# The low part of w_up: a ScalarE negation and an accumulating transfer in place of a VectorE subtraction

## The chip, the cores and the metric

The kernel runs on one core of one Trainium2 chip. The metric is the device time of one launch in microseconds (us), lower is better. Before the change it is 2234.87 us, the median of 3 runs (2234.61 to 2236.42).

## What is computed

One layer of a hybrid decoder on 512 tokens of width 2048, all in float32. Cut to what matters here:

```python
h = rmsnorm(x, norm1_w)
proj = h @ w_in                      # split among three groups of mixers
y = concat(stick_breaking(6 heads), short_conv(4 groups), gated_delta(6 heads))
x = x + y @ w_out
h2 = rmsnorm(x, norm2_w)
x = x + square(relu(h2 @ w_up)) @ w_down     # w_up: 2048 x 8192, w_down: 8192 x 2048
return rmsnorm(x, final_norm_w)
```

## The kernel before, in words

**Products of split numbers.** Every float32 operand of a large product is split into a high part (rounded to float32r by a ScalarE copy) and a low part (the rest: VectorE subtracts the high part from the operand). A product is then three matmuls into one PSUM bank, in `mm3` (L106): high times high (L108), high weight times low activation (L109), low weight times high activation (L110).

**Loading weights.** `wload` (L96 to L104) does this for w_in, w_out and w_up, in pieces of 128 x 512, 256 KB each, 2 KB in each partition: a transfer on SP's queue into `raw` (L99), the copy on ScalarE that writes `whi` (L102), the subtraction on VectorE that writes `wlo` (L103). Each of the three tiles has four buffers. So the high part for a piece can be written when the piece four before it has been through L109, and `raw` is free again when L103 has read it. The whole of `wload` is put 400 places forward in the planner's priority.

**Stages.** From 0 to about 545 us of the span: the first projections and the gated delta heads. To about 760 us: attention. To about 911 us: x + y @ w_out (L734 to L754), 16 columns of 4 pieces each; per column one GpSimd addition of squares (L750) is made towards the norm. Then w_up: a row tile f of 128 features needs four pieces (`up_chunk`, L760), each 12 matmuls; after the fourth, VectorE (L775) and ScalarE (L776) take the squared ReLU. The first 16 pieces (L782 to L789) come one right after the other, but for the transposes of `turn` (L729) and the sum over partitions of the squares (L785), which needs the last L750. Then, until about 2180 us, each block of 16 pieces is interleaved with 14 units of the w_down product (L913 to L919): a piece, a unit, a piece, a unit, and two pieces without a unit at the end of a block. A unit is a Strassen-like product of 12 matmuls as well; its weights `q` come on SP's queue (L839, 512 KB each), are combined on VectorE (L848) and split on ScalarE (L806) and VectorE (L807); its results are added on VectorE (L876). The last 53 us are the last block of w_down, the final norm and the output.

**Order.** Each engine runs its instructions in an order fixed when the program is built. The planner orders them by a simulated timeline and by the priorities. SP's queue carries the loads of `raw` and of `q`. GpSimd (POOL) carries the additions of L750 in the w_out stage, the last multiplications (L952), and nothing between 955 and 2180 us.

Of the kernel before, what the change touches and what calls it, by code (L numbers as in the profile page):

```python
# [11 lines left out]
F32 = mybir.dt.float32  # L12
F32R = mybir.dt.float32r
AF = mybir.ActivationFunctionType
ALU = mybir.AluOpType

P = 128
# [10 lines left out]
CHUNK_KT = 4  # L28
# [25 lines left out]
def trunk(ctx, tc, xT, wv1, wv2, wa, wo, wu, wd, vec, wf, out, dbg=None):  # L54
    nc = tc.nc
    V, S, G, PE = nc.vector, nc.scalar, nc.gpsimd, nc.tensor
# [15 lines left out]
    def mmps():  # L72
        pool, bufs = pool_of_mm
        return pool.tile([P, 512], F32, name="mm", tag="mm", bufs=bufs)

    def xps(tag):
        pool, bufs = pool_of[tag]
        return pool.tile([P, 512], F32, name=tag, tag=tag, bufs=bufs)
# [8 lines left out]
    def tmp(n=512):  # L87
        return per.tile([P, n], F32, name="tmp", tag="tmp", bufs=4)
# [4 lines left out]
    def f32t(shape, name):  # L93
        return per.tile(shape, F32, name=name)

    def wload(src, n, prio=None):  # L96
        with tc.high_priority(WPRIO if prio is None else prio):
            raw = per.tile([P, 512], F32, name="raw", tag="raw", bufs=4)
            nc.sync.dma_start(out=raw[:, :n], in_=src)  # L99
            hi = per.tile([P, 512], F32R, name="whi", tag="whi", bufs=4, align_bytes=256)  # L100
            lo = per.tile([P, 512], F32R, name="wlo", tag="wlo", bufs=4, align_bytes=256)
            S.copy(out=hi[:, :n], in_=raw[:, :n])  # L102
            V.tensor_tensor(out=lo[:, :n], in0=raw[:, :n], in1=hi[:, :n].bitcast(F32), op=ALU.subtract)  # L103
        return hi, lo  # L104

    def mm3(p, lh, ll, rh, rl, first, last, more=False):  # L106

        PE.matmul(p, lhsT=lh, rhs=rh, start=first, stop=False, skip_group_check=more)  # L108
        PE.matmul(p, lhsT=lh, rhs=rl, start=False, stop=False, skip_group_check=more)  # L109
        PE.matmul(p, lhsT=ll, rhs=rh, start=False, stop=last, skip_group_check=more)  # L110

    def gemm(src, acts, ts=slice(0, T)):

        p = mmps()[:, :ts.stop - ts.start]
        nk = len(acts)
        for c in range(0, nk, CHUNK_KT):
            hi, lo = wload(src[:, c:c + CHUNK_KT, :].rearrange("p k f -> p (k f)"), CHUNK_KT * P)
            for k in range(CHUNK_KT):
                s = slice(k * P, (k + 1) * P)
                a = acts[c + k]  # L120
                mm3(p, hi[:, s], lo[:, s], a[:, 0, ts], a[:, 1, ts], c + k == 0, c + k == nk - 1)
        return p
# [59 lines left out]
    for k in range(KT):  # L182
        hi, lo = wload(wv1[:, k, :], 268, 0)
        xr = big_pool.tile([P, 512], F32, name="xr", tag="xr", bufs=3)
        nc.sync.dma_start(out=xr, in_=xT[:, k, :])
        a = big()
        w = col(C_N1 + k)
        S.activation(out=a[:, 0], in_=xr, func=AF.Copy, scale=w)
        V.scalar_tensor_tensor(out=a[:, 1], in0=xr, scalar=w, in1=a[:, 0].bitcast(F32),
                               op0=ALU.mult, op1=ALU.subtract)  # L190
        for b in range(NB):
            s = slice(b * P, (b + 1) * P)
            mm3x = v1p[b][:, :268]
            PE.matmul(mm3x, lhsT=a[:, 0, s], rhs=hi[:, :268], start=k == 0, stop=False)
            PE.matmul(mm3x, lhsT=a[:, 0, s], rhs=lo[:, :268], start=False, stop=False)
            PE.matmul(mm3x, lhsT=a[:, 1, s], rhs=hi[:, :268], start=False, stop=k == KT - 1)
        if k == 0:
            S.activation(out=acc, in_=xr, func=AF.Square)
        else:
            sq = tmp()  # L200
            if k % 2:
                V.tensor_tensor(out=sq, in0=xr, in1=xr, op=ALU.mult)
            else:
                S.activation(out=sq, in_=xr, func=AF.Square)
            G.tensor_tensor(out=acc, in0=acc, in1=sq, op=ALU.add)
        xw.append(a)
    R = pt([P, 512], "R")
    p = xps("r")
# [3 lines left out]
    p = xps("r")  # L212
# [44 lines left out]
    def v_stage(i):  # L257
        pp = [mmps(), mmps()]
        for c in range(0, KT, 2):
            hi, lo = wload(wv2[i - 1][:, c:c + 2, :].rearrange("p k f -> p (k f)"), 512)  # L260
            for kk in range(2):
                k = c + kk
                ws = slice(kk * 256, kk * 256 + 256)
                for b in range(NB):
                    s = slice(b * P, (b + 1) * P)
                    o = pp[b // 2][:, (b % 2) * 256:(b % 2) * 256 + 256]
                    PE.matmul(o, lhsT=xw[k][:, 0, s], rhs=hi[:, ws], start=k == 0 and b % 2 == 0, stop=False)  # L267
                    PE.matmul(o, lhsT=xw[k][:, 0, s], rhs=lo[:, ws], start=False, stop=False)  # L268
                    PE.matmul(o, lhsT=xw[k][:, 1, s], rhs=hi[:, ws], start=False, stop=k == KT - 1 and b % 2 == 1)  # L269
        vt[i] = v_evac(lambda b: pp[b // 2][:, (b % 2) * 256:(b % 2) * 256 + 256], sp_pool)  # L270
# [32 lines left out]
    p = xps("r")  # L303
# [430 lines left out]
    for m in range(KT):  # L734
        xr = big_pool.tile([P, 512], F32, name="xr", tag="xr", bufs=3)
        nc.sync.dma_start(out=xr, in_=xT[:, m, :])
        p = gemm(wo[m], yh)
# [22 lines left out]
    def up_chunk(f, c, st):  # L760

        if c == 0:
            st["p"] = mmps()
        p = st["p"]
        hi, lo = wload(wu[f][:, c * CHUNK_KT:(c + 1) * CHUNK_KT, :].rearrange("p k f -> p (k f)"), CHUNK_KT * P)
        for k in range(CHUNK_KT):
            s = slice(k * P, (k + 1) * P)
            a = xw2[c * CHUNK_KT + k]
            mm3(p, hi[:, s], lo[:, s], a[:, 0], a[:, 1], c + k == 0, c == KT // CHUNK_KT - 1 and k == CHUNK_KT - 1)
        if c == KT // CHUNK_KT - 1:  # L770
            g = f // HK
            if f % HK == 0:
                hp[g] = late.tile([P, HK, 512], F32, name="hp", tag="hp", bufs=3)
            t = tmp()
            V.scalar_tensor_tensor(out=t, in0=p, scalar=0.0, in1=Rb, op0=ALU.max, op1=ALU.mult)  # L775
            S.activation(out=hp[g][:, f % HK], in_=t, func=AF.Square)  # L776
# [5 lines left out]
    for n in range(FBLK * NCH):  # L782
        if n == 1:
            p = xps("r")
            PE.matmul(p, lhsT=ones, rhs=acc2, start=True, stop=True)  # L785
            rsqrt_exp(Rb, p, 1.0 / D, None)
        if n == 2:
            turn(KT - 2)
        up_chunk(n // NCH, n % NCH, ust)  # L789
# [123 lines left out]
    for b in range(nblk - 1):  # L913
        for n in range(FBLK * NCH):
            up_chunk((b + 1) * FBLK + n // NCH, n % NCH, ust)
            if n < 14:
                if n % 7 == 0:
                    dst = {}
                unit(b, n // 7, PROD[n % 7], dst)  # L919
# [110 lines left out]
```

## Time and profile before

| | |
|---|---|
| median of 3 runs | 2234.87 us (2234.61 to 2236.42) |
| the profiled execution: own time | 2235.26 us |
| its span, first to last instruction | 2233.3 us |
| TensorE (PE) busy | 2206.4 us, 99% |
| VectorE (DVE) busy | 1618.9 us, 72% |
| ScalarE (ACT) busy | 943.9 us, 42% |
| GpSimd (POOL) busy | 90.8 us, 4% |
| mean granted clock of TensorE | 0.997 |

Busy times are sums over the span. PE is matmuls, PEld the loading of their weights, which runs beside them. In a row of a group of instructions, the number after x counts them, the two after the first bar are their busy time in us and the mean of one in ns, and after the second bar stands the idle time of the engine just before them and what ended most of it. A releaser written `<-PE mm L109` means that the engine waited for that.

### The profile page before, as it was taken

How to read it: one execution, taken by the hardware profiler on the slowest of the kernel's cores; microseconds unless marked ns; L12 is line 12 of the kernel's file. 1: busy time of each engine (PE TensorE's matmuls, PEld its weight loads, DVE VectorE, ACT ScalarE, POOL GpSimd, SP SyncE). 2: the span in 40 equal slices, each digit the busy share in tenths (PEclk: the TensorE clock that was granted, in tenths of full speed). 3: DMA queues.
4: the chain of work that ended last, by engine and by line, in shares of the span. 5: the costliest groups of instructions: out<-in, count | busy, mean ns of one | idle time of the engine just before them, and what ended most of it. 6: DMA issues, size and time to landing. Idle time of an engine off the chain costs nothing.

```text
span 2233.3 us, 28056 instructions
## 1 busy us (share of the span) xinstructions
PE 2206.4 (99%) x10394; PEld 1831.8 (82%) x10394; DVE 1618.9 (72%) x2262; ACT 943.9 (42%) x1563; POOL 90.8 (4%) x126
## 2 busy tenths in 40 slices
PE   7999999999999999999999999999999999999998
PEld 6887888878988888888888888888888888888886
DVE  7787999754657633477787777778878878778774
ACT  5645655433435433433343333333333433333334
POOL 4000000000000111000000000000000000000003
PEclk9999999999999999999999999999999999999999
DMA  6332323322222333433333333343333332333432
GB/s 185 98 94 83 87 80 91 86 79 85 81 85 81 108 114 113 141 98 117 97 101 115 92 109 109 90 118 99 90 123 94 99 113 90 113 104 93 118 111 79
DMA packets 112505, 227.06 MB, mean 102 GB/s; under 512 B 18448, under 2 KB 20624, under 8 KB 112368
## 3 DMA queue, kind: packets, MB, share of 16 engines
q1 hardware_dynamic: 112368, 225.26, 34.2%
q8 instruction: 82, 1.34, 0.3%
q14 instruction: 55, 0.45, 0.1%
HBM read 218.53 MB, written 6.68 MB: 101 GB/s over the span
## 4 chain that ended last, share of the span: by engine, by line
PE 93%; DVE 4%; DMA 1%; issue 1%; ACT 1%; SPq 0%; ACTq 0%; DVEq 0%
PE mm L108 20%; PE mm L109 20%; PE mm L110 20%; PE pp L108 9%; PE pp L110 9%; PE pp L109 9%; DVE wlo L103 1%; PE mm L269 1%; PE mm L268 1%; PE mm L267 1%; DVE Yq L432 1%; DVE tq L430 1%; DVE cv L337 0%; DMA xr<-in_xT_dram 0%; PE i L391 0%
## 5 line engine op out<-in xcount | busy, mean ns | idle before, releaser
L102 ACT CAST whi<-raw 128x512 fp32r<-128x512 f32 (+1 forms) x544 | 333.1, 613 | 622.6 <-PE mm L109 579.3
L103 DVE TENSOR_TENSOR wlo<-raw,whi 128x512 fp32r<-128x512 f32 (+1 forms) x544 | 374.1, 688 | 246.3 <-ACT whi L102 234.0
L876 DVE TENSOR_TENSOR xq<-pp,xq 128x1024 f32<-128x1024 f32 x240 | 290.8, 1222 | 203.0 <-PE pp L110 200.5
L108 PE MATMUL mm<-big,whi 128*128 128x512 f32 x1024 | 404.7, 396 | 0.0
L110 PE MATMUL mm<-big,wlo 128*128 128x512 f32 x1024 | 403.5, 394 | 0.0
L109 PE MATMUL mm<-big,whi 128*128 128x512 f32 x1024 | 403.3, 394 | 0.0
L108 PE MATMUL mm<-xw,whi 128*128 128x512 f32 x1024 | 398.8, 389 | 0.0
L110 PE MATMUL mm<-xw,wlo 128*128 128x512 f32 x1024 | 398.4, 389 | 0.0
L109 PE MATMUL mm<-xw,whi 128*128 128x512 f32 x1024 | 398.4, 389 | 0.0
L806 ACT CAST W<-q 128x1024 fp32r<-128x1024 f32 x210 | 220.7, 1051 | 402.1 <-PE pp L110 398.4
L108 PE MATMUL pp<-W,A 128*128 128x512 f32 x840 | 326.8, 389 | 0.0
L109 PE MATMUL pp<-W,A 128*128 128x512 f32 x840 | 326.8, 389 | 0.0
L110 PE MATMUL pp<-W,A 128*128 128x512 f32 x840 | 326.8, 389 | 0.0
L807 DVE TENSOR_TENSOR W<-q,W 128x1024 fp32r<-128x1024 f32 x210 | 255.5, 1217 | 2.6 <-ACT W L806 2.6
L109 PEld LDWEIGHTS mm<-big,whi 128*128 128x128 f32 x1024 | 193.0, 188 | 39.4 <-DVE big L710 0.3
L110 PEld LDWEIGHTS mm<-xw,wlo 128*128 128x128 f32 x1024 | 192.3, 188 | 40.0
L110 PEld LDWEIGHTS mm<-big,wlo 128*128 128x128 f32 x1024 | 192.9, 188 | 39.2
L109 PEld LDWEIGHTS mm<-xw,whi 128*128 128x128 f32 x1024 | 192.1, 188 | 40.1 <-issue 0.2
L108 PEld LDWEIGHTS mm<-xw,whi 128*128 128x128 f32 x1024 | 192.1, 188 | 39.9 <-issue 0.2
L108 PEld LDWEIGHTS mm<-big,whi 128*128 128x128 f32 x1024 | 192.9, 188 | 38.7 <-ACT big L709 0.3
L108 PEld LDWEIGHTS pp<-W,A 128*128 128x128 f32 x840 | 157.7, 188 | 32.9
L109 PEld LDWEIGHTS pp<-W,A 128*128 128x128 f32 x840 | 157.7, 188 | 32.7
(264 smaller groups left out, 2117.3 us busy)
## 6 DMA issues: line engine op xcount, KB each, us to landing
raw<-in_wu_dram SPq DMA_DIRECT2D x256, 256.0 KB
q<-in_wd_dram SPq DMA_DIRECT2D x128, 512.0 KB
raw<-in_wa_dram SPq DMA_DIRECT2D x192, 256.0 KB
raw<-in_wo_dram SPq DMA_DIRECT2D x64, 256.0 KB
xr<-in_xT_dram SPq DMA_DIRECT2D x32, 256.0 KB
raw<-in_wv_dram SPq DMA_DIRECT2D x16, 256.0 KB
out_dram<-xq SPq DMA_DIRECT2D x16, 256.0 KB
raw<-in_wv_dram SPq DMA_DIRECT2D x16, 134.0 KB
```

The lines of the kernel that those rows point to most:

```text
L102: S.copy(out=hi[:, :n], in_=raw[:, :n])
L103: V.tensor_tensor(out=lo[:, :n], in0=raw[:, :n], in1=hi[:, :n].bitcast(F32), op=ALU.subtract)
L108: PE.matmul(p, lhsT=lh, rhs=rh, start=first, stop=False, skip_group_check=more)
L109: PE.matmul(p, lhsT=lh, rhs=rl, start=False, stop=False, skip_group_check=more)
L110: PE.matmul(p, lhsT=ll, rhs=rh, start=False, stop=last, skip_group_check=more)
L267: PE.matmul(o, lhsT=xw[k][:, 0, s], rhs=hi[:, ws], start=k == 0 and b % 2 == 0, stop=False)
L268: PE.matmul(o, lhsT=xw[k][:, 0, s], rhs=lo[:, ws], start=False, stop=False)
L269: PE.matmul(o, lhsT=xw[k][:, 1, s], rhs=hi[:, ws], start=False, stop=k == KT - 1 and b % 2 == 1)
L430: V.tensor_tensor(out=tv, in0=B[:, 0:i, i:i + 1].broadcast_to([16, i, n]), in1=Y[:, i:i + 1, i:32].broadcast_to([16, i, n]), op=ALU.mult)
L806: S.copy(out=o[:, 0], in_=src)
L807: V.tensor_tensor(out=o[:, 1], in0=src, in1=o[:, 0].bitcast(F32), op=ALU.subtract)
L876: V.tensor_tensor(out=x, in0=p, in1=x, op=ALU.add)
```

## The change

For w_up alone, `wload` gets a flag. With it, ScalarE writes minus the high part into `wlo`, and a transfer on POOL's queue reads the same 256 KB of weights from device memory a second time and adds them to `wlo` where it lies. The subtraction on VectorE stays for the other weights.

```diff
-    def wload(src, n, prio=None):
+    def wload(src, n, prio=None, by_dma=False):
 ...
             S.copy(out=hi[:, :n], in_=raw[:, :n])
-            V.tensor_tensor(out=lo[:, :n], in0=raw[:, :n], in1=hi[:, :n].bitcast(F32), op=ALU.subtract)
+            if by_dma:
+                S.mul(out=lo[:, :n], in_=hi[:, :n].bitcast(F32), mul=-1.0)
+                nc.gpsimd.dma_start(out=lo[:, :n], in_=src, accum_op=ALU.add)
+            else:
+                V.tensor_tensor(out=lo[:, :n], in0=raw[:, :n], in1=hi[:, :n].bitcast(F32), op=ALU.subtract)
 ...
-        hi, lo = wload(wu[f][:, c * CHUNK_KT:(c + 1) * CHUNK_KT, :].rearrange("p k f -> p (k f)"), CHUNK_KT * P)
+        hi, lo = wload(wu[f][:, c * CHUNK_KT:(c + 1) * CHUNK_KT, :].rearrange("p k f -> p (k f)"), CHUNK_KT * P,
+                       by_dma=True)
```

## Rows read from the trace of the kernel before

**Rows 1.** The page: busy time of each engine, and the shares of the chain of work that ended last.
```profile
PE 2206.4 (99%) x10394; PEld 1831.8 (82%) x10394; DVE 1618.9 (72%) x2262; ACT 943.9 (42%) x1563; POOL 90.8 (4%) x126
PE 93%; DVE 4%; DMA 1%; issue 1%; ACT 1%; SPq 0%; ACTq 0%; DVEq 0%
```

**Rows 2.** The windows view, one line for a stage: start and end, length, busy us of each engine with its instructions, then the granted clock of TensorE, the mean busy share of the 16 DMA engines, and GB/s.
```profile
0.00:545.00 545.00, 526.96 (x2714) 431.83 (x2715) 420.62 (x882) 279.33 (x579) 41.96 (x71) 0.99 0.34 97
545.00:760.00 215.00, 215.00 (x1194) 188.06 (x1193) 138.01 (x195) 96.67 (x164) 8.13 (x24) 1.00 0.28 83
760.00:910.00 150.00, 150.00 (x690) 124.48 (x689) 59.80 (x85) 59.16 (x112) 18.85 (x14) 1.00 0.40 118
910.00:955.00 45.00, 45.00 (x202) 36.98 (x201) 22.37 (x29) 18.95 (x31) 1.29 (x1) 1.00 0.48 152
955.00:2180.00 1225.00, 1225.00 (x5406) 1014.34 (x5405) 956.76 (x1040) 467.47 (x624) 0.00 (x0) 1.00 0.35 104
2180.00:2233.00 53.00, 44.47 (x195) 36.15 (x193) 21.30 (x35) 22.34 (x54) 20.61 (x16) 0.97 0.22 80
```

**Rows 3.** Groups of PE's instructions from 955 to 2180 us: the matmul that reads the low part, and one of a unit of w_down.
```profile
L110 PE MATMUL mm<-xw,wlo 128*128 128x512 f32 x962 | 374.2, 389 | 0.0
L110 PE MATMUL pp<-W,A 128*128 128x512 f32 x840 | 326.8, 389 | 0.0
```

**Rows 4.** Groups of VectorE's instructions from 955 to 2180 us, the costliest four.
```profile
L876 DVE TENSOR_TENSOR xq<-pp,xq 128x1024 f32<-128x1024 f32 x240 | 290.8, 1222 | 203.0 <-PE pp L110 200.5
L807 DVE TENSOR_TENSOR W<-q,W 128x1024 fp32r<-128x1024 f32 x207 | 251.8, 1217 | 0.0
L103 DVE TENSOR_TENSOR wlo<-raw,whi 128x512 fp32r<-128x512 f32 x238 | 163.4, 687 | 47.8 <-ACT whi L102 47.8
L848 DVE TENSOR_TENSOR q<-q 128x1024 f32<-128x1024 f32 x116 | 141.8, 1223 | 2.0
```

**Rows 5.** Groups of ScalarE's instructions from 955 to 2180 us, the costliest two.
```profile
L806 ACT CAST W<-q 128x1024 fp32r<-128x1024 f32 x207 | 217.5, 1051 | 398.4 <-PE pp L110 398.4
L102 ACT CAST whi<-raw 128x512 fp32r<-128x512 f32 x237 | 147.2, 621 | 308.1 <-PE mm L109 308.1
```

**Rows 6.** POOL's instructions from 545 us to the end, its two longest kinds.
```profile
L952 POOL TENSOR_TENSOR xq<-xq,wf 128x512 f32<-128x512 f32 x16 | 20.6, 1291 | 1292.5 <-ACT tmp L951 1292.5
L750 POOL TENSOR_TENSOR acc<-acc,tmp 128x512 f32<-128x512 f32 x15 | 20.1, 1343 | 162.6 <-ACT tmp L749 162.5
```

**Rows 7.** The chain of work that ended last, in order of time (start, us, what): the transfers in it around the start and in the gated delta heads. The first two are loads of 256 KB, the last one moves 16 KB.
```profile
3.60 4.41 DMA xr<-in_xT_dram
...
146.66 2.61 DMA raw<-in_wa_dram
...
157.15 1.67 DMA Xc<-sy
```

**Rows 8.** DMA issues as SP's queue shows them: durations in ns (min/median/max).
```profile
L99 SPq DMA_DIRECT2D raw<-in_wu_dram x234: 327/328/412, 955.1 to 2142.0; - x117
```

**Rows 9.** The timeline where w_out ends and w_up begins: PE's first matmul of two pieces, ScalarE's writing of the high parts, the transposes and the sum, POOL's last addition.
```profile
905.72 0.39 PE L108 MATMUL mm<-big,whi 128*128 128x512 f32 x1
...
908.43 0.39 PE L108 MATMUL mm<-big,whi 128*128 128x512 f32 x1
908.45 0.62 ACT L102 CAST whi<-raw 128x512 fp32r<-128x512 f32 x1 [2.10 <-PE mm L109]
...
911.13 0.62 ACT L102 CAST whi<-raw 128x512 fp32r<-128x512 f32 x1 [2.06 <-PE mm L109]
...
913.47 1.29 POOL L750 TENSOR_TENSOR acc<-acc,tmp 128x512 f32<-128x512 f32 x1 [10.24 <-ACT tmp L749]
...
918.17 1.02 PE L785 MATMUL r<-acc,ones 128*128 128x512 f32 x2
```

**Rows 10.** The timeline in the interleaved stage: ScalarE's writing of three high parts in a row, and the first matmul of the piece of w_up between the first two.
```profile
1399.81 0.62 ACT L102 CAST whi<-raw 128x512 fp32r<-128x512 f32 x1 [1.40 <-PE mm L109]
...
1402.55 0.39 PE L108 MATMUL mm<-xw,whi 128*128 128x512 f32 x1
...
1405.25 0.62 ACT L102 CAST whi<-raw 128x512 fp32r<-128x512 f32 x1 [1.40 <-PE mm L109]
...
1410.69 0.62 ACT L102 CAST whi<-raw 128x512 fp32r<-128x512 f32 x1 [0.87 <-PE mm L109]
```

**Rows 11.** The DMA view of 955 to 2180 us: the queue's packets, MB and share of the time of 16 engines, and the issues with their sizes.
```profile
q1 hardware_dynamic: 51696, 126.90, 35.0%
...
q<-in_wd_dram SPq DMA_DIRECT2D x123, 512.0 KB
raw<-in_wu_dram SPq DMA_DIRECT2D x234, 256.0 KB
```

**Rows 12.** The same view of 910 to 955 us.
```profile
q1 hardware_dynamic: 3024, 6.82, 47.6%
...
raw<-in_wu_dram SPq DMA_DIRECT2D x16, 256.0 KB
q<-in_wd_dram SPq DMA_DIRECT2D x5, 512.0 KB
```

**Rows 13.** What SP's queue waited for from 955 to 2180 us: us in total, times, longest.
```profile
SPq L99 <- DVE wlo L103: 669.7, 234, 5.8
SPq L839 <- DVE W L807: 401.0, 120, 5.1
```

**Rows 14.** The end of the chain of work that ended last.
```profile
2224.80 0.24 PE mm L110
2225.07 0.70 DVE xq L950
2225.79 0.73 ACT tmp L951 x2
2226.74 0.30 ACT rs L135
2227.30 0.72 ACT xq L972
2228.02 0.61 ACTq L1024
```

## The prediction, made before the changed kernel was run

> **What bounds the kernel now.** I read the page first: TensorE is busy 99% of the span and makes up 93% of the chain that ended last; VectorE has 4% of the chain, though it is busy 72% of the span [rows 1]. An average over the span doesn't say where those 4% lie, so I cut the span into stages [rows 2]. The reader is to see two things. All of PE's idle time lies before 545 us (545 - 527 = 18 us) and after 2180 us (53 - 44.5 = 8.5 us). From 545 to 2180 us, which holds every piece of w_up, PE is busy 45.00 of 45.00 us and 1225.00 of 1225.00 us, at full granted clock. The list of PE's groups says the same: no idle time ahead of L110, which reads the low part, and none ahead of the units' matmuls [rows 3]. So in the stage that the change touches, PE's own work sets the end. From 955 to 2180 us its pace is 1225 / 5406 = 0.227 us a matmul, 12 x 0.2266 = 2.72 us for a piece or a unit; from one piece to the next in the timeline 908.43 - 905.72 = 2.71 us [rows 9].
>
> **What is removed.** 256 subtractions of 687 ns, 176 us of VectorE; the 238 in the interleaved stage are 163.4 of its 956.8 busy us [rows 2, 4]. Worth on the path: 0, since PE does not wait there. Its cover is PE, and no edit here touches PE's work. VectorE falls from 78% to about 65% of that stage, and that gives nothing back. SP's loads of `raw`, which waited 234 times for the subtraction [rows 13], will wait for ScalarE's reading instead and start earlier, by at most the 5.8 us of the longest such wait; `raw` is not late now, so this too is worth 0.
>
> **What is added on ScalarE.** 256 multiplications of 128 x 512 at the price of the copy of that shape, 621 ns [rows 5]: 159 us in all, 148 of them in the interleaved stage, where ScalarE goes from 467.5 to about 615 of 1225 us, 50% [rows 2]. In the first 45 us it goes from 19 to 29. It has room, and a multiplication stands right behind its copy. Behind it on ScalarE wait the splits of L806, 0.62 us later than now; they idle 398 us in all for PE [rows 5]. Worth: 0.
>
> **What is added on POOL's queue and the DMA engines.** 256 transfers that read, add and write. The trace has no accumulating transfer and no transfer on POOL's queue, so I bound both. Three things can be too slow.
>
> *Issue.* Lower end: what SP needs, 0.33 us [rows 8]. Upper end: POOL's longest kind of instruction, 1.34 us [rows 6]. I take 1.34, the row of the same engine. POOL has nothing else from 955 to 2180 us [rows 2], so 1.34 us per piece hides behind a period of 1225 / 234 = 5.24 us, and behind the 2.72 us of the first 16 pieces.
>
> *Landing.* Lower end: the 16 KB piece, 1.67 us. The row of the same size and source is 2.61 us, the longest load of that size 4.41 us [rows 7]. Adding needs the old value read and the sum written, so I take it as two passes one after the other: 2 x 2.61 = 5.2 us; upper end 2 x 4.41 = 8.8 us. With the issue 6.6 us (2.0 to 10.2).
>
> What covers it: a low part is needed four pieces after its buffer came free. In the first 16 pieces: the copy that starts at 908.45 fills the buffer of the piece that began at 905.72 [rows 9]; the multiplication ends at 908.45 + 2 x 0.62 = 909.7; the fourth piece on begins at 905.72 + 4 x 2.72 = 916.6 and its first L110 0.45 us later. That leaves 7.3 us for 6.6, a margin of 0.7. In the interleaved stage copies are 5.44 us apart [rows 10], so the same sum gives 7.35 + 4 x 2.72 = 18.2 us, and where two pieces without a unit fall in, 7.35 + 2 x 2.72 = 12.8 us: more than even the upper end. So latency can bite in the first 16 pieces only.
>
> *Throughput.* In the interleaved stage 126.9 MB took 35.0% of the DMA engines [rows 11]: 0.350 x 1225 / 126.9 = 3.38 us a MB, 0.89 us of all 16 engines for one 256 KB load. One pass more per piece adds 0.89 / 5.24 = 17 points, two 34 (35 to 69%). The engines are full at (1 - 0.35) x 5.24 / 0.89 = 3.8 passes. In the 45 us before, 48% are taken [rows 12] and 23.4 us are free; 16 transfers of one pass need 14.2 us, of two passes 28.4, 5 us too many. But 5 of the loads there are of `q`, 512 KB each and some 8.9 us together, which no unit needs before 955 us, so two passes fit if these give way. I take two passes here too, and a cost of 0. The price of adding in the transfer stands in one page only, the Trainium skill's "Collectives: The Full Stack", section "The bandwidth ceiling: the fold count and why AG ≠ RS ≠ AR": a reducing transfer reads two sources and runs at half the rate of a copy; by it a piece would cost an estimated 1.8 us of the engines, and the sum would stay what it is.
>
> *POOL's order.* POOL's last addition ends at 914.8 us and the sum that reads it starts on PE at 918.2, 3.4 us later [rows 9]. Two transfers ahead of it on POOL cost 2.7 us and hide; a third would cost PE 0.6 us. Taken: 0.
>
> **Sum.** 0 - 0 + 0 on the profiled execution's own 2235.26 us, which stands 0.39 us above the median of the runs. I forecast 2235.3 us. A measurement of this kernel can tell a change of about 0.2%, 4.5 us, from none.
>
> **Rivals.**
>
> *The start of w_up stalls (slower).* The place is the first 16 pieces, the price by the upper end 10.2 - 7.3 = 2.9 us for each round of four buffers, four rounds: 11.6 us, 2247 us. It decides from a landing of 6.0 us on (7.3 - 1.34). For it: the margin is 0.7 us, and the DMA engines are busiest there. Against it: the row of the same load is 2.61 us. Chance 0.15.
>
> *The DMA engines become the bound (slower).* Above 3.8 passes per transfer the interleaved stage runs at their pace: at five passes 0.35 x 5.24 + 5 x 0.89 = 6.3 us per piece, 1.0 us more, 234 times: about +240 us, 2475 us. No row shows why one add should cost five copies, and none shows what it costs. Chance 0.07.
>
> *VectorE holds POOL up (slower).* VectorE is busy 78% of the interleaved stage with instructions of up to 1.22 us [rows 2, 4]. If POOL had to wait for one of these both when it starts and when it ends its issue, 2.4 us come on top of 6.6: 9.0, 1.7 us short in four rounds, 6.8 us: 2242 us. Against it: two waits of the longest kind are needed each time, VectorE is busy half of the first 45 us only, and nothing here shows POOL and VectorE blocking each other. Chance 0.05. The Trainium skill's "SBUF — State Buffer", section "SBUF: two separate sides", warns of just this: transfers issued from GpSimd starve while VectorE holds the port pair that they share. Its section "Who interferes with whom" takes it back for two-input `tensor_tensor`, and that is the kind of all four rows of VectorE shown here; no run yet shows either.
>
> *VectorE's relief pays (faster).* To gain 4.5 us it would have to come out of the 8.5 us that PE idles after 2180 us, since the 18 us before 545 come before any w_up. There the chain ends in one VectorE addition of 0.70 us, ScalarE steps and the output [rows 14], none of it L103. A reordering there is worth under 1 us (2234.5). Chance of over 4.5 us (2230): 0.04.
>
> **How the numbers follow.** Forecast (PE full throughout, 2235.3, itself from 2232 to 2239): 0.69. Rivals: 0.15, 0.07, 0.05, 0.04. Slower by over 0.2%: 0.15 + 0.07 + 0.05 = 0.27; faster 0.04; within 0.2% 0.69. The range takes in the forecast's own spread below, and above it the two nearer slow cases at their price: 2232 to 2248. It leaves out the DMA bound and the faster case, 0.11.
>
> **What would show it.** Right: PE busy throughout 910 to 2180 us, L110's rows still with no idle time; VectorE's busy time 176 us less, ScalarE's 159 us more; DMA share of the interleaved stage between 0.52 and 0.69; no wait of PE for the new transfer. Wrong: PE waiting for `wlo` between 911 and 960 us (first rival), in every block, with a DMA share near 1 (second), or transfers whose issue on POOL is over 1.34 us beside VectorE's instructions (third). A wait in the blocks with a low DMA share would mean that a single transfer takes more than 12.8 us from end of multiplication to use, which none of my rows reaches.

## The result, and the profile after

The median of 20 runs after is 2238.56 us, that of 20 runs before on the same chips 2235.52 us: a ratio of 1.0013, 95% interval 1.0007 to 1.0019. That is a small loss, 3 us, inside the 0.2% that the forecast called "no change", but not zero. The profiled execution took 2238.55 us with a span of 2236.9 us, 3.6 us more than before. The ratios, here and below, leave out two executions that ran much longer than the rest, one of 4502 us of the kernel with the transfer in the first 16 pieces only and one of 2712 us of the kernel before.

The page after: busy time of each engine, and the chain that ended last.

```profile
PE 2208.5 (99%) x10394; PEld 1833.6 (82%) x10394; DVE 1466.7 (66%) x2006; ACT 1096.1 (49%) x1819; POOL 314.3 (14%) x382
PE 93%; DVE 3%; DMA 1%; issue 1%; ACT 1%; SPq 0%; POOL 0%; ACTq 0%; DVEq 0%; POOLq 0%
```

VectorE has lost 152 us against [rows 1], ScalarE has gained 152, POOL 224, and the end has not come nearer. (Busy time counts the overlap of two instructions once, and one often starts some 0.1 us before the one ahead of it ends. So the 256 subtractions take off less than their 176 us, and the 256 negations of 632 ns add less than their 162 us.) The windows view of the same stages as [rows 2] shows where the 3.6 us are (columns as there: PE, PEld, DVE, ACT, POOL, clock, DMA share, GB/s):

```profile
0.00:545.00 545.00, 528.63 (x2716) 434.18 (x2717) 421.15 (x882) 279.38 (x579) 41.96 (x71) 0.99 0.34 97
545.00:760.00 215.00, 215.00 (x1194) 188.06 (x1193) 138.10 (x194) 96.67 (x164) 8.18 (x24) 1.00 0.28 83
760.00:910.00 150.00, 150.00 (x691) 124.48 (x690) 57.51 (x81) 61.10 (x115) 21.24 (x17) 1.00 0.41 121
910.00:955.00 45.00, 42.02 (x185) 33.52 (x184) 12.43 (x13) 26.44 (x44) 13.84 (x16) 1.00 0.96 228
955.00:2180.00 1225.00, 1225.00 (x5406) 1014.36 (x5405) 812.79 (x797) 607.04 (x859) 208.43 (x239) 1.00 0.68 156
2180.00:2236.00 56.00, 47.88 (x210) 38.98 (x209) 24.73 (x40) 25.46 (x59) 20.64 (x16) 0.96 0.23 84
```

The reader is to see one line: from 910 to 955 us PE is busy 42.02 of 45 us, where it was full before, and the DMA engines are at 0.96 instead of 0.48. The 1225 us that follow are as full as they were. What PE waited for from 905 to 975 us (us in total, times, longest), and where it did so (the first matmuls that read the low part of three pieces, among the first nine of the sixteen):

```profile
PE mm L115 <- DMA wlo<-in_wu_dram: 3.0, 3, 1.9
```

```profile
926.29 0.39 PE L114 MATMUL mm<-xw,whi 128*128 128x512 f32 x1
927.46 0.50 PE L115 MATMUL mm<-xw,wlo 128*128 128x512 f32 x1 [0.78 <-DMA wlo<-in_wu_dram]
927.79 0.40 PE L113 MATMUL mm<-xw,whi 128*128 128x512 f32 x1
928.03 0.40 PE L114 MATMUL mm<-xw,whi 128*128 128x512 f32 x1
...
933.28 0.39 PE L114 MATMUL mm<-xw,whi 128*128 128x512 f32 x1
935.59 0.50 PE L115 MATMUL mm<-xw,wlo 128*128 128x512 f32 x1 [1.92 <-DMA wlo<-in_wu_dram]
...
938.44 0.50 PE L115 MATMUL mm<-xw,wlo 128*128 128x512 f32 x1 [0.29 <-DMA wlo<-in_wu_dram]
```

(L113 to L115 are the matmuls that were L108 to L110, L103 the copy, L105 the negation, L106 the transfer, L812 the splits of q, L781 the ReLU.) The transfers themselves, as the view of the tile `wlo` and the DMA view show them: duration of the issue on POOL in ns, time from issue to landing, and the queues' packets, MB and share of 16 engines, first from 955 to 2180 us, then from 910 to 955. q0 carries POOL's transfers, q1 SP's loads.

```profile
L106 POOL DMA_DIRECT2D wlo<-in_wu_dram x256: 858/865/1008, 904.1 to 2166.5; - x128
DMA to landing us min/median/max: 4.0/4.5/9.4
```

```profile
q1 hardware_dynamic: 51759, 126.77, 34.0%
q0 software_dynamic: 34560, 62.93, 33.7%
...
q0 software_dynamic: 2070, 3.75, 52.9%
q1 hardware_dynamic: 2831, 6.48, 42.7%
```

One transfer needs 0.337 x 1225 / 240 = 1.72 us of the 16 engines, and a plain load of its size, at the mean price of q1's loads, 0.340 x 1225 / 126.77 x 0.262 = 0.86 us: the transfer needs twice as much. It is issued in 0.87 us and lands 4.5 us after the issue began (6.5 at most from 955 us on), which the interleaved stage hides. Of the first pieces, the three that were issued between 916 and 930 us took 7.4 to 9.4 us, the others 4.4 to 6.8.

Why those three? Two things happen between 917 and 931 us. They show in the timelines of SP, ScalarE and POOL:

```profile
917.39 3.29 SPq L845 DMA_DIRECT2D q<-in_wd_dram  x5
```

```profile
920.59 0.62 ACT L103 CAST whi<-raw 128x512 fp32r<-128x512 f32 x1 [0.27 <-PE mm L114]
921.24 0.63 ACT L105 ACTIVATE wlo<-whi 128x512 fp32r<-128x512 f32 x1
923.91 1.05 ACT L812 CAST W<-q 128x1024 fp32r<-128x1024 f32 x1 [2.04 <-DMA q<-in_wd_dram]
924.87 0.62 ACT L103 CAST whi<-raw 128x512 fp32r<-128x512 f32 x1
926.15 1.05 ACT L812 CAST W<-q 128x1024 fp32r<-128x1024 f32 x1 [0.67 <-DMA q<-in_wd_dram]
927.11 0.62 ACT L105 ACTIVATE wlo<-whi 128x512 fp32r<-128x512 f32 x1
```

```profile
918.01 0.86 POOL L106 DMA_DIRECT2D wlo<-in_wu_dram  x1 [2.12 <-ACT wlo L105]
922.23 0.86 POOL L106 DMA_DIRECT2D wlo<-in_wu_dram  x1 [3.36 <-ACT wlo L105]
928.15 0.88 POOL L106 DMA_DIRECT2D wlo<-in_wu_dram  x1 [5.06 <-ACT wlo L105]
```

At 917.4 us SP issues five loads of `q`, 512 KB each. The transfer issued at 918.01 runs beside them and lands at 927.4: the first wait. And the planner put splits of q, which wait for those loads, into ScalarE's order: one ahead of the eighth piece's copy, one between its copy and its negation, and a third in the same place of the ninth piece. So the negation of the eighth piece ends at 927.7 us (927.11 + 0.62), some 3 us late, its transfer is issued at 928.15 instead of about 925, and it lands too late as well: the second, longest wait. The ninth piece's transfer is late behind it.

### The profile page after: what moved, and what is told of

Same layout as the page of the kernel before. It is cut to its first block, busy times and chain, and to the rows that moved or that the text cites. A ratio compares the mean times of both kernels' runs of the same rounds, so it can differ in the third digit from the quotient of the medians.

```text
span 2236.9 us, 28585 instructions
## 1 busy us (share of the span) xinstructions
PE 2208.5 (99%) x10394; PEld 1833.6 (82%) x10394; DVE 1466.7 (66%) x2006; ACT 1096.1 (49%) x1819; POOL 314.3 (14%) x382
## 3 DMA queue, kind: packets, MB, share of 16 engines
q8 instruction: 82, 1.34, 0.3%
## 4 chain that ended last, share of the span: by engine, by line
PE 93%; DVE 3%; DMA 1%; issue 1%; ACT 1%; SPq 0%; POOL 0%; ACTq 0%; DVEq 0%; POOLq 0%
PE mm L113 20%; PE mm L115 20%; PE mm L114 20%; PE pp L115 9%; PE pp L113 9%; PE pp L114 9%; PE mm L274 1%; PE mm L273 1%; PE mm L272 1%; DVE wlo L108 1%; DMA xr<-in_xT_dram 1%; DVE Yq L437 0%; DVE tq L435 0%; PE i L396 0%; DVE big L194 0%
## 5 line engine op out<-in xcount | busy, mean ns | idle before, releaser
L103 ACT CAST whi<-raw 128x512 fp32r<-128x512 f32 (+1 forms) x544 | 333.2, 613 | 611.8 <-PE mm L114 568.6
L113 PE MATMUL mm<-big,whi 128*128 128x512 f32 x1024 | 404.7, 396 | 0.0
L115 PE MATMUL mm<-big,wlo 128*128 128x512 f32 x1024 | 403.6, 394 | 0.0
L115 PE MATMUL mm<-xw,wlo 128*128 128x512 f32 x1024 | 398.7, 389 | 3.0 <-DMA wlo<-in_wu_dram 3.0
L113 PE MATMUL mm<-xw,whi 128*128 128x512 f32 x1024 | 398.5, 389 | 0.0
L106 POOL DMA_DIRECT2D wlo<-in_wu_dram x256 | 223.4, 872 | 1039.9 <-ACT wlo L105 1039.6
L812 ACT CAST W<-q 128x1024 fp32r<-128x1024 f32 x210 | 221.2, 1053 | 294.1 <-PE pp L115 268.4
L113 PE MATMUL pp<-W,A 128*128 128x512 f32 x840 | 326.8, 389 | 0.0
L115 PE MATMUL pp<-W,A 128*128 128x512 f32 x840 | 326.8, 389 | 0.0
L108 DVE TENSOR_TENSOR wlo<-raw,whi 128x512 fp32r<-128x512 f32 (+1 forms) x288 | 199.6, 694 | 179.1 <-ACT whi L103 167.7
L115 PEld LDWEIGHTS mm<-xw,wlo 128*128 128x128 f32 x1024 | 192.2, 188 | 44.2 <-DMA wlo<-in_wu_dram 4.2
L115 PEld LDWEIGHTS mm<-big,wlo 128*128 128x128 f32 x1024 | 193.0, 189 | 39.2
L113 PEld LDWEIGHTS mm<-big,whi 128*128 128x128 f32 x1024 | 192.9, 188 | 38.7 <-ACT big L714 0.3
L113 PEld LDWEIGHTS mm<-xw,whi 128*128 128x128 f32 x1024 | 192.0, 188 | 39.7
L113 PEld LDWEIGHTS pp<-W,A 128*128 128x128 f32 x840 | 157.8, 188 | 32.9
```

Source lines behind the costliest of these rows:

```text
L106: nc.gpsimd.dma_start(out=lo[:, :n], in_=src, accum_op=ALU.add)
L812: S.copy(out=o[:, 0], in_=src)
```

## The experiments

A measure that is free of what the early stages do from run to run is the time from PE's first matmul with a low part of w_up to its first matmul of a unit, both from the views of the tiles, in the one profiled execution of each kernel: 47.6 us before (911.6 to 959.2) and 51.5 us after (911.1 to 962.6). The time from the start of the first unit matmul to that of the last one of the same line (959.2 to 2174.4, 962.6 to 2177.8) is 1215.2 us in both. The medians of the experiments stand against 2235.1 to 2235.2 us of the kernel before on the same chip; the recorded ratios differ from the quotients of the medians by up to 0.0004.

| kernel | median us | ratio, 95% interval | start of w_up | units |
|---|---|---|---|---|
| after | 2238.56 | 1.0013 (1.0007 to 1.0019) | 51.5 | 1215.2 |
| subtraction in the first 16 | 2235.38 | 1.0003 (0.9994 to 1.0012) | 47.6 | 1215.1 |
| transfer in the first 16 only | 2237.52 | 1.0011 (1.0002 to 1.0020) | 50.1 | 1215.1 |
| q loads held back | 2243.07 | 1.0037 (1.0025 to 1.0050) | 51.6 | 1218.9 |
| q splits held back | 2237.78 | 1.0013 (1.0005 to 1.0022) | 49.5 | 1215.1 |
| no transfer | 2235.16 | 1.0001 (0.9992 to 1.0010) | 47.6 | 1215.2 |
| a second transfer in the blocks | 2239.19 | 1.0018 (1.0009 to 1.0027) | 50.5 | 1215.2 |
| the change at w_in instead | 2245.86 | 1.0052 (1.0040 to 1.0065) | 47.6 | 1215.2 |

**Where does the loss sit? The transfer for all but the first 16 pieces.**

```diff
-                       by_dma=True)
+                       by_dma=f >= FBLK)
```

> The first 16 pieces of w_up keep the subtraction; the other 240 get the transfer. Theory A (the loss of 3 us sits in the first 16 pieces, where PE waits three times for the transfer; the interleaved stage costs nothing): the time of the kernel before, 2235.5 us within 1 us, PE busy 45.0 of the 45 us from 910 us on, the DMA share there back near 0.5, the interleaved stage unchanged with a DMA share of 0.68. Rival B (every transfer costs a little, 3 us over 256): 240/256 of the loss stays, 2238.4 us.

No loss is left. From 910 to 955 and from 955 to 2180 us:

```profile
910.00:955.00 45.00, 45.00 (x202) 36.99 (x201) 20.54 (x26) 20.76 (x34) 4.03 (x4) 1.00 0.55 163
955.00:2180.00 1225.00, 1225.00 (x5406) 1014.38 (x5405) 817.35 (x803) 609.16 (x862) 206.23 (x237) 1.00 0.66 155
```

PE is full, with 240 transfers in the blocks and the DMA engines at 0.66. Theory A holds, an equal cost for every transfer does not: its 2238.4 us lie above the interval.

**The mirror: the transfer for the first 16 pieces only** (`by_dma=f < FBLK`).

> The mirror of it: only the first 16 pieces get the transfer. Theory A: the whole loss stays, 2238.5 us, PE waits for wlo in the same three places, about 3 us; from 962 us on nothing is different from the kernel before, DMA share 0.35. Rival B: 16/256 of the loss, 2235.7 us.

2237.52 us. (The interval still just holds rival B's 2235.7; the experiment above rules it out.) PE waits for the transfer twice, 2.0 us, instead of three times, 3.0 us, and the start takes 2.5 us longer than before instead of 3.9:

```profile
910.00:955.00 45.00, 43.05 (x191) 34.70 (x190) 13.81 (x15) 25.63 (x44) 12.59 (x14) 1.00 0.92 226
955.00:2180.00 1225.00, 1225.00 (x5406) 1014.36 (x5405) 955.86 (x1038) 466.90 (x623) 0.00 (x0) 1.00 0.35 104
```

Most of the loss comes from 16 of the 256 transfers, in two of the three places: at the sixth and the eighth piece. How much such a start costs varies: the three kernels whose first 16 pieces are alike (this one, the full change, and the one with a second transfer in the blocks) lose 2.5, 3.9 and 2.9 us there, and in all three PE waits at the sixth and the eighth piece.

**Are the loads of q the trigger? Hold them back.** ScalarE writes one element in each partition of the first five q buffers from the third row tile's result, so the loads wait for it.

```diff
+        if held[0] < 5:
+            held[0] += 1
+            S.copy(out=q[:, 0, 0:1], in_=hp[1][:, 0, 0:1])
         nc.sync.dma_start(out=q, in_=wd[b, j, kh, d])
```

> The full change, but the first five loads of w_down (q, 512 KB each) are held back until the third row tile of w_up is done: ScalarE writes one element of each q buffer from that tile's result ahead of the load. Theory A1 (the start stalls because these five loads share the DMA engines with the transfers, and because the planner puts the splits of q between ScalarE's copy and its negation): both are gone, no wait of PE for wlo, the transfer that took 9.4 us to land takes under 6: 2235.5 us within 1 us. Rival C (two passes and the load of raw alone fill the DMA engines at one piece per 2.72 us, with or without q): PE still waits 2 to 4 us, 2238 us. A danger that is neither: q may come too late for the first unit and PE waits there instead, for W and not for wlo.

The time missed: 2243.07 us. The stage did what A1 said as long as q was held, and the danger that was named came true, though the releaser is another one:

```profile
920.00:947.00 27.00, 27.00 (x121) 22.33 (x120) 2.77 (x4) 15.12 (x26) 7.81 (x9) 1.00 0.88 179
947.00:963.00 16.00, 10.29 (x45) 7.85 (x43) 5.35 (x6) 8.68 (x17) 3.71 (x5) 0.99 1.02 292
```

```profile
PE pp L113 <- DVE tmp L781: 4.5, 1, 4.5
PE mm L115 <- DMA wlo<-in_wu_dram: 1.3, 1, 1.3
```

```profile
958.88 1.23 DVE L859 TENSOR_TENSOR q<-q 128x1024 f32<-128x1024 f32 x1 [1.64 <-DMA q<-in_wd_dram]
...
962.29 0.68 DVE L781 SCALAR_TENSOR_TENSOR tmp<-mm,Rb 128x512 f32<-128x512 f32 x1
```

```profile
960.00:970.00 10.00, 6.88 (x25) 5.62 (x26) 10.00 (x13) 6.58 (x10) 1.61 (x2) 0.83 0.69 166
```

From 920 to 947 us, pieces follow each other at PE's full pace with a transfer each, the engines are at 0.88, and PE never waits: rival C falls. When q is issued at 947.5 us the share reads 1.02, which is full, and PE waits for a transfer again, 1.3 us: the collision has moved with q. (Whether the engines themselves or the device memory behind them were what was short, no run separates.) The 4.5 us are another wait: VectorE's L781 stood behind the combination of the late q (L859 in this kernel) in VectorE's order, and the first unit, by the profile's releaser, behind L781. So q cannot simply give way: it is wanted soon after. In the table this kernel's two columns belong together, since the planner put ten of the twelve matmuls of the piece ahead of the first unit behind that unit. Together the start and the units are 7.7 us longer than before: 1.6 for the wait for `wlo`, 4.7 for the other one, and 1.4 because, after those 4.5 us without work, PE's granted clock was lower (a mean of 0.83 in the ten us from 960) and the unit's first matmuls followed each other at 0.43 us instead of 0.227.

**Is it ScalarE's order or the engines? Hold only the splits back.**

```diff
             o = w_tile()
+            if held[0] < 3:
+                held[0] += 1
+                S.copy(out=o[:, 0, 0, 0:1], in_=hp[1][:, 0, 0:1])
             split(o, src)
```

> The full change; q is loaded as early as before, but ScalarE's first three splits of q are held back until the third row tile of w_up is done, so that no split stands between copy and negation. Theory A1 with both parts: the first wait (0.9 us, a transfer that was issued on time and took 9.4 us to land) stays, the later ones (about 2.2 us, transfers that were issued 3 us late) go: 2236.5 us. Rival D (ScalarE's order alone): no wait is left, 2235.5 us. Rival E (the DMA engines alone): all three waits stay, 2238.5 us.

The eighth piece's transfer is now issued on time, 2.8 us after the seventh's instead of 5.9, and of the three waits only the first is left:

```profile
922.99 0.86 POOL L106 DMA_DIRECT2D wlo<-in_wu_dram  x1 [3.36 <-ACT wlo L105]
925.78 0.88 POOL L106 DMA_DIRECT2D wlo<-in_wu_dram  x1 [1.94 <-ACT wlo L105]
```

```profile
927.05 0.39 PE L114 MATMUL mm<-xw,whi 128*128 128x512 f32 x1
928.65 0.50 PE L115 MATMUL mm<-xw,wlo 128*128 128x512 f32 x1 [1.21 <-DMA wlo<-in_wu_dram]
```

So both parts of A1 are there: the later waits were ScalarE's order, the first one is the engines. The start takes 49.5 us, 1.9 more than before, against 2.5 to 3.9 in the three kernels that have the splits in the way. (A later matmul on a low part starts 0.24 us late, at 942.64 us; it is part of the 1.9.) The median, 2237.78 us, is 1.3 us above what was expected, its ratio is that of the full change, and the interval holds A1's 2236.5 us and rival E's 2238.5: the time doesn't tell these two apart, only the one trace does.

**Is VectorE's relief worth anything by itself?** The line of the transfer is deleted.

> Leaves out the addition: ScalarE writes minus the high part, and no transfer follows, so the low part lacks the weights. VectorE's relief and ScalarE's load stay, the cost of the transfer is gone. Theory F (VectorE's relief is worth nothing, since PE is never idle in this stage): 2235.5 us within 1.5 us, VectorE's busy time about 1467 us as with the full change. Rival G (the relief is worth something that the transfer hides): 2231 us or less.

2235.16 us, 1.0001. VectorE is at 1466.4 us and ScalarE at 1096.1, as with the full change, and PE is full from 545 to 2180 us: the relief is worth nothing and ScalarE's 256 negations cost nothing, within the 0.1% of the interval. What makes the loss comes with the transfer. But this kernel takes away both parts of A1 at once, since without the transfer the planner put no split of q between a copy and its negation.

**How much room do the blocks have? A second transfer from the 17th piece on.**

```diff
                 nc.gpsimd.dma_start(out=lo[:, :n], in_=src, accum_op=ALU.add)
+                if twice:
+                    nc.gpsimd.dma_start(out=raw[:, :n], in_=src, accum_op=ALU.add)
```

> From the 17th piece on each piece gets a second accumulating transfer of 256 KB, into raw after it has been read; the result does not change. One transfer took 33.7% x 1225 / 240 = 1.72 us of the 16 DMA engines, the loads 1.8 us per piece, and the period is 5.24 us. Theory H (only the engines' time counts, and 1.8 + 2 x 1.72 = 5.2 us just fills the period): a DMA share of 0.97 to 1.0 and landings of 8 us or more; the time between no loss and 3% (2236 to 2305 us), PE waiting for wlo or W in the blocks. Rival I (the landing is dominated by a fixed latency and the engines are far from full): no loss, share below 0.9, landing still near 4.5 us.

No loss in the blocks: 1215.2 us of units, PE full. The windows and DMA views of 955 to 2180 us and the landings of `wlo`:

```profile
955.00:2180.00 1225.00, 1225.00 (x5407) 1014.32 (x5406) 812.58 (x796) 607.00 (x859) 419.27 (x478) 1.00 0.95 207
```

```profile
q0 software_dynamic: 69110, 125.84, 60.9%
q1 hardware_dynamic: 51842, 126.93, 34.0%
```

```profile
DMA to landing us min/median/max: 4.3/7.0/9.8
```

The share rises to 0.95 and the median landing from 4.5 to 7.0 us: rival I is out, since the engines' time does count. Theory H is right in kind, at the harmless end of its range; the waits of PE in the blocks that it named did not come, and the share and the landing are a little below its numbers: the second transfer takes (0.609 - 0.337) x 1225 / 240 = 1.39 us, not 1.72. Even a landing of 9.8 us fits under the 12.8 us that the forecast had worked out for the blocks. Of the 4.3 us by which this execution's span is longer than that of the kernel before, 2.9 are in the start, and 0.7 each ahead of w_up and behind the units; no run says whether these two repeat.

**Where VectorE is on the chain: the change at w_in.** The 72 pieces of q, k and v for the gated delta heads get it (`by_dma=True` in the three `gemm` calls there), w_up keeps the subtraction.

> The same change at another place: w_up keeps the subtraction, and the 72 pieces of w_in for q, k and v of the gated delta heads get ScalarE's negation and the transfer. There VectorE is busy 85 to 91% of the time and L103 stands on the chain, but PE idles only 6.6 us between 100 and 545 us. Theory J (relief pays only where PE waits, and at most what it waits; pieces follow each other at 2.72 us, so some transfers come late): between 3 us faster and 6 us slower, 2232 to 2242 us. Rival K (VectorE is what holds this stage, 72 subtractions of 0.69 us come off it): 5 us or more faster, below 2231 us, with VectorE's share there down by 50 us.

2245.86 us, outside what either theory gave. The windows view up to 100 us, first of the kernel before, then of this one, and POOL's first transfers:

```profile
0.00:100.00 100.00, 88.55 (x471) 75.41 (x472) 72.45 (x106) 61.95 (x128) 28.85 (x36) 1.00 0.50 145
```

```profile
0.00:50.00 50.00, 33.41 (x220) 29.41 (x220) 37.45 (x49) 30.86 (x62) 28.41 (x32) 0.99 0.68 195
50.00:100.00 50.00, 49.90 (x213) 41.15 (x214) 17.80 (x30) 35.81 (x73) 15.35 (x20) 0.95 0.83 175
```

```profile
42.59 2.81 POOL L106 DMA_DIRECT2D wlo<-in_wa_dram  x3
```

And from 0 to 545 us:

```profile
0.00:545.00 545.00, 519.18 (x2676) 425.80 (x2677) 369.59 (x800) 310.70 (x636) 103.62 (x143) 0.99 0.54 131
```

```profile
PE mm L115 <- DMA wlo<-in_wa_dram: 4.7, 3, 3.8
```

Most of the loss falls at the very first piece. Its negation was done at 40.4 us, but POOL issued the transfer at 42.59, behind an addition of squares, and it landed 7.5 us later, beside SP's loads of `raw` and `xr`. PE's first matmul on a low part started at 50.1 us instead of 42.3; 3.8 us of this are a wait for the transfer. After it PE's matmuls followed each other at 0.43 us instead of 0.227 until 55.4 us, and the granted clock from 50 to 100 us is 0.95. At 100 us PE has done 433 matmuls instead of 471, and 38 are some 8.6 us at its full pace.

From 100 to 545 us it does 2244, against 2245 in the kernel before, though VectorE is busy 314 us there instead of 348. So K's gain doesn't show: with VectorE a tenth lighter, this stage goes no faster. (No run has the relief there without the transfer, which would be the clean test.) In the next stage the first matmul on a low part starts 11.5 us later than before (570.9 instead of 559.4); where the 3 us that are not from the first 100 came from was not settled. J was right that some transfers would come late, and too small in its price.

## Why the prediction came out as it did

**What bounds the kernel, and the value of the relief: right, and shown.** PE is full from 545 to 2180 us but for the start of w_up, and without any transfer the lighter VectorE gives 2235.16 us. The faster rival had no place to come from.

**ScalarE: price right, order wrong.** A negation takes 0.63 us (0.62 forecast), and its 256 are free by themselves. But "a multiplication stands right behind its copy" failed where it mattered: in the eighth and the ninth piece the planner put a split of q between them, and these waited for q. (In the sixth it was a short copy of the transposes, 0.37 us.) Holding the splits back took the later waits away.

**Issue and landing: forecast too dear.** 0.87 us instead of 1.34, and 4.5 us from the start of the issue instead of 6.6. Against 7.3 us of cover that leaves 2.8 us of margin, not 0.7. Latency by itself stalls nothing, as the stretch without q shows.

**Throughput: two passes, right; "two passes fit if these give way", wrong.** This is the step that failed. The interleaved stage was forecast at 69% and came to 0.68. For the 45 us before, the sum found 5 us of engine time too many and then dropped them because no unit needs q so early. The loads of q did not give way: the DMA engines served both queues together, at 0.96, one transfer's landing went to 9.4 us, and, with the delays in ScalarE's order, the start took 3.9 us longer. Forced to give way, q was late for the first unit, and PE waited 4.5 us there. So the first rival (the start stalls) is what happened, and the forecast's own sign of being wrong, PE waiting for `wlo` between 911 and 960 us, was there. The rival was given a chance of 0.15 and a price of 11.6 us, by a landing of 10.2 us in each of four rounds. Three transfers came near it (7.4 to 9.4 us), because of the load on the engines and not by themselves, and the true price is a third. With it the kernel stays within 0.2%. The forecast of "no change" holds by size and not by its sum of 0, and that is luck: nothing in the prediction kept a stalled start under 0.2%.

**The other rivals.** The DMA bound would have needed 3.8 passes; with a second transfer in the blocks PE still never waited at a share of 0.95. VectorE did not hold POOL up: 256 issues took between 858 and 1008 ns beside a VectorE that is busy two thirds of the stage. The Trainium skill's "SBUF — State Buffer" has both sides of this, and the trace agrees with its section "Who interferes with whom", by which two-input `tensor_tensor` was not seen to stall transfers: POOL's issue kept its 858 to 1008 ns. The Trainium skill's "Collectives: The Full Stack", section "The bandwidth ceiling: the fold count and why AG ≠ RS ≠ AR", has the reducing step of a ring of cores at half a copy's rate; the 1.72 against 0.86 us measured here fit the same factor, though for another kind of transfer.

## What to carry to other kernels

An engine that is busy 72% of the time is worth nothing to relieve where another one is full; the windows by stage say that before anything is built, and deleting the added cost shows it after. When transfers are added, do the sum of the DMA engines' time for the shortest stage and not only for the longest: 5 us too many in 45 us came with a start 3.9 us longer, part of it by the engines and part by instructions that waited for the same loads in ScalarE's order, while 1225 us at 0.68, even at 0.95, cost nothing. And a load that isn't needed yet does not step aside: to count on that, one has to hold it back by a dependency, and then check that it isn't late.

## What the runs showed of the hardware that was not expected

An accumulating transfer of 256 KB into on-chip memory takes no more of the 16 engines than two plain loads of that size (1.72 us against 0.86 for one), and a second one per piece adds only 1.39 us. The DMA engines ran at a share of 0.95 for 1225 us, moving 207 GB/s, with the landing no worse than 9.8 us. A wait of PE costs more than the idle time that the view gives: the matmul before the first wait started at 926.29 us and the one behind it at 927.46, 0.94 us more than the usual 0.227, where the view counts 0.78 from the end of the first; the next few then follow at 0.33 and 0.24 us. So 3.0 us of waits made the start 3.9 us longer. After the two longest waits of the experiments, 4.5 us (q loads held back) and 3.8 us (the change at w_in), six to twelve matmuls followed each other at 0.43 us, about half the pace.
